# Building the S5 tables beside the first feed-forward block: T1 transposed by its filled half, its zeros written to memory once, and the table work paced anew

## The chip, the cores and the metric

The kernel runs on one core of one Trainium2 chip. The metric is device time in microseconds (us) of one execution. A core has TensorE (PE, matrix products; PEld is its weight load), VectorE (DVE), ScalarE (ACT), GpSimd (POOL) and SyncE (SP); each takes its instructions strictly in the order in which they were written for it. Transfers between memory and the core are issued on the queues of SP, ACT and POOL and share 16 DMA engines.

## The reference

A decoder trunk of two layers on 256 tokens of width 1024. Each layer is half a SwiGLU feed-forward block, a token mixer, and another half feed-forward block, all with residuals; the mixer of layer 0 is an S5 state-space layer, that of layer 1 is block-sparse attention.

```python
h = h + 0.5 * swiglu(rms_norm(h, ffn_norm[l, 0]), w_gate[l, 0], w_up[l, 0], w_down[l, 0])
h = h + mixer_l(rms_norm(h, mix_norm[l]))       # l = 0: s5_mixer, l = 1: moba_mixer
h = h + 0.5 * swiglu(rms_norm(h, ffn_norm[l, 1]), w_gate[l, 1], w_up[l, 1], w_down[l, 1])

def swiglu(h, w_gate, w_up, w_down):            # 1024 -> 2816 -> 1024
    return (silu(h @ w_gate) * (h @ w_up)) @ w_down

def s5_mixer(h, ...):                           # 64 groups of 16 channels, 64 complex states a group
    u = h @ w_in
    lam = exp((a_re + i a_im) * dt)
    bb = ((lam - 1) / (a_re + i a_im)) * (b_re + i b_im)
    st[t] = lam * st[t - 1] + bb @ u[t]         # per group, over the tokens
    y = real(c @ st) + d_skip * u
    g = gelu(y); g = g * sigmoid(g @ w_glu)
    return g @ w_out
```

Everything is float32. Of `s5_mixer`, what depends on the weights alone (powers of `lam`, their products with `b` and with `c`) is a set of tables, and this change touches how these are built.

## The kernel before

**The stages.** The phases run in the order f00 (the first feed-forward block), s5, f01, f10, moba, f11. A float32 product is done as three products of a reduced type: each weight `w` is split into `whi` (a rounded copy, by ACT, L86) and `wlo = w - whi` (by DVE, L87), activations likewise, and `mm3` (L398 to L401) adds up the three. In f00 a large matmul streams 512 columns.

**The weight stream.** `Stream` (L37 to L131) holds the order of all weights in units of 1 MB. SP loads a unit into one of three `raw` buffers (L176 for gate and up weights, L182 for down weights and others); `split` cuts a unit into two halves of `whi` and `wlo`, for which there are nine buffers. A `raw` buffer is loaded again once its second half is split. In f00 the units come by columns j of 256 hidden channels: gate and up of columns 0 and 1 (two units each), then down of column j - 1 behind gate and up of column j. `pump` calls, written between the matmuls, split ahead. SP's transfers take turns on eight semaphores, so that one can't be issued before the eighth before it has landed; POOL's do the same on eight of their own.

**Tables beside f00.** `tables` (L615) is a Python generator. While f00 is being written down, `fill(dt)` (called once per 0.7 units, three large matmuls) moves a clock `slot` and lets the generator emit work. The tables are built for 8 blocks of 8 groups. Per block b:

- `muls` and `sums` (DVE) make `zc`, products of `b` and `c` with powers of `lam`, with `cb` as their input (`b_all` makes B's part, `c_tr` transposes C on PE and ACT copies it to `cb`).
- `spread` (L850) copies `zc` on ACT to `TT` and to `MPs`, where the two groups of a pair lie in separate halves of partitions and columns and the other halves are zero, and stores `TT` to memory (`dB`, L859, on POOL). `TT` has one buffer.
- `t3_tab` (L877): 16 small matmuls, copies to `kt`, four stores to `dB` (L892, POOL).
- `t1_tab` (L863), called twice: four 128x128 transposes of `MPs` on PE (L866), a copy `t1` from PSUM on ACT (L868), one store of 256 KB to `dA` (L869, POOL). Half of what is transposed and stored is zero.

The order of it is set by lists. `LOADS` has the clock values at which the loads of B (`ld_b4`, eight pieces of 64 KB in 64-byte runs, L649) and of C (`ld_c2`, four pieces of 128 KB, L654) are put on SP's queue. `work` holds DVE's pieces with costs in units; a credit grows by `DENSE` units per unit of the clock, and a piece is emitted when the credit covers it. The PE pieces of a block (`t3_tab`, `t1_tab`, `t1_tab`) follow `LAG` = 12 units after `spread`, `PACE` = 4.0 units apart (`later`).

**After the tables.** When f00 is done, the rest of the tables is emitted, and SP loads `dA`, `dE` and `dB` of three blocks into `TA`, `TE`, `TB` (L951 to L959). The first of these waits for the last eight stores of POOL's queue. `TA` is read by the matmuls of L1009 in the S5 stage.

Of the kernel before, what the change touches and what calls it, by code (L numbers as in the profile page):

```python
# [10 lines left out]
F32 = mybir.dt.float32  # L11
F32R = mybir.dt.float32r
AF = mybir.ActivationFunctionType
# [16 lines left out]
AO = (68, 68, 68, 68)  # L30
OO = 68

LOADS = (16, 16.5, 17, 17.5, 18, 18.5, 19, 19.5, 22, 24, 26, 28)
C_AT, E_AT, B_AT, DENSE, LAG, PACE, AGE = 44, 26, 36, 0.46, 12, 4.0, 8.0


class Stream:  # L37
# [83 lines left out]
def trunk_kernel(ctx: ExitStack, tc, x, ffn_norm, ffn_w_gate, ffn_w_up, ffn_w_down, mix_norm,  # L121
# [3 lines left out]
    nc = tc.nc  # L125
# [13 lines left out]
    def psR():  # L139
        return pp.tile([128, 512], F32, name="pR", tag="R", bufs=2)  # L140
# [96 lines left out]
    ident = cst[:, 0:128]  # L237
# [7 lines left out]
    h = [h2[:, t, :] for t in range(2)]  # L245
# [374 lines left out]
    def tables(tp):  # L620

        V, P = nc.vector, nc.gpsimd

        def T(name, *shape):
            return tp.tile([128] + list(shape), F32, name=name)

        def tt(o, a, b, op, eng=V):
            eng.tensor_tensor(o, a, b, op=op)
# [4 lines left out]
            else:  # L633
                eng.tensor_scalar(o, a, s1, s2, op0=op0, op1=op1)

        MPs = [T(f"mp{k}", 2, 4, 4, 2, 16) for k in range(2)]
        TT = T("tt", 2, 4, 4, 2, 16)
        kts = [T(f"kt{k}", 7, 2, 16) for k in range(2)]
        cf7 = T("cf7", 7, 2)
        for k, n in enumerate(range(15, 1, -2)):  # L640
            for i in range(2):
                P.memset(cf7[:, k, i:i + 1], (-1.0) ** ((n - i) // 2) / math.factorial(n - i))
        for m in MPs + [TT] + kts:
            P.memset(m, 0.0)
        bn = [tp.tile([128, 32, 16], F32, name="bn", tag="n0", bufs=2) for i in range(2)]
        cn = tp.tile([128, 1280], F32, name="cn", tag="n1", bufs=2)[:, 0:1024].rearrange("p (i a c) -> p i a c", i=2, c=64)
        def ld_b4(i, c):
            b = (s5_b_re, s5_b_im)[i]
            nc.sync.dma_start(bn[i][:, 8 * c:8 * c + 8], bass.AP(tensor=b.tensor, offset=b.offset + 16384 * c,  # L649
                                                                 ap=[[16, 128], [2048, 8], [1, 16]]))  # L650

        def ld_c2(i, a):
            c = (s5_c_re, s5_c_im)[i]
            nc.sync.dma_start(cn[:, i, 4 * a:4 * a + 4], bass.AP(tensor=c.tensor, offset=c.offset + 32768 * a,  # L654
                                                                 ap=[[64, 128], [8192, 4], [1, 64]]))

        loads = [lambda i=i, c=c: ld_b4(i, c) for c in range(4) for i in range(2)]
        loads += [lambda i=i, a=a: ld_c2(i, a) for a in range(2) for i in range(2)]
        yield
        dtb = tp.tile([32, 2, 64], F32, name="dtb")  # L660
        nc.scalar.activation(dtb, ldt[:, :, None].to_broadcast([32, 2, 64]), AF.Exp)
# [1 line left out]
        ps = psR()  # L663
# [26 lines left out]
        q, y, y2, e0, e1, den = (T(n, 32) for n in ("q", "y", "y2", "e0", "e1", "den"))  # L690
# [20 lines left out]
        ps = psR()  # L711
# [118 lines left out]

        HALF = [slice(0, 64), slice(64, 128)]

        ZC = {}

        def muls(b, k):
            tt((z0, z1)[k].rearrange("p (x s n) -> p x s n", s=4, n=16),
# [3 lines left out]
        def sums(b, i):  # L840

            if i == 0:
                ZC[b] = tp.tile([128, 2, 2, 4, 80], F32, name="zc", tag="n1", bufs=2)
                P.tensor_copy(ZC[b][:, 0, :, :, 0:16].rearrange("p i q n -> p (i q) n"),
                              cb[:, b, 0].rearrange("p i q n -> p (i q) n"))
            u, v = (z.rearrange("p (m i q x) -> p m i q x", m=2, i=2, q=4) for z in (z0, z1))
            x, y = ((u[:, :, 0], v[:, :, 1]), (u[:, :, 1], v[:, :, 0]))[i]
            tt(ZC[b][:, :, i, :, 16:80], x, y, (OP.subtract, OP.add)[i])

        def spread(b):  # L850

            d_diag(b)
            tv, mv = (o.rearrange("p i q s g n -> p (i q) s g n") for o in (TT, MPs[b % 2]))
            zv = ZC[b].rearrange("p m i q (s n) -> p m (i q) s n", n=16)
            for g, r in enumerate(HALF):
                nc.scalar.activation(tv[r, :, :, g, :], zv[r, 0, :, 1:5], AF.Copy)
                nc.scalar.activation(mv[r, :, :, g, :], zv[r, 1, :, 1:5], AF.Copy)
            for i in range(2):
                nc.gpsimd.dma_start(dB[b][:, 512 * i:512 * i + 512].rearrange("p (q x) -> p q x", q=4),  # L859
                                    TT[:, i].rearrange("p q t g n -> p q (t g n)"))  # L860

        def t1_tab(b, i):
            t1 = tp.tile([128, 4, 128], F32, name="t1", tag="n0", bufs=2)  # L863
            ps = psR()
            for q4 in range(4):
                nc.tensor.transpose(ps[:, q4 * 128:(q4 + 1) * 128],  # L866
                                    MPs[b % 2][:, i, q4].rearrange("p s g n -> p (s g n)"), ident)
            nc.scalar.activation(t1.rearrange("p q c -> p (q c)"), ps, AF.Copy)  # L868
            nc.gpsimd.dma_start(dA[b][:, i * 512:(i + 1) * 512], t1.rearrange("p q c -> p (q c)"))  # L869

        DG = {}

        def d_diag(b):
            DG[b] = tp.tile([128, 2, 16], F32, name="dg", bufs=2)
            P.tensor_scalar(DG[b], i32, dT[:, b:b + 1], None, op0=OP.mult)

        def t3_tab(b):  # L877

            kt = kts[b % 2]
            ps = psR()  # L880
            zc = ZC.pop(b)
            for i in range(2):
                for qq in range(4):
                    mm(ps[32 * qq:32 * qq + 32, 0:64], MPs[b % 2][:, i, qq, 3].rearrange("p g n -> p (g n)"),
                       zc[:, 0, i, qq, 0:64], start=i == 0, stop=i == 1)
            pk = ps[:, 0:64].rearrange("p (t c) -> p t c", c=16)
            for g in range(2):
                nc.scalar.activation(kt[:, 3:7, g, :], pk, AF.Identity, scale=gm[:, g:g + 1])
            P.tensor_tensor(kt[:, 3], kt[:, 3], DG.pop(b), op=OP.add)
            for s in range(4):  # L890
                o = dB[b][32 * s:32 * s + 32, 1024:1536].rearrange("r (q x) -> q r x", q=4)
                nc.gpsimd.dma_start(o, kt[:, 3 - s:7 - s].rearrange("p t g n -> p (t g n)"))  # L892
# [12 lines left out]

        def add_spread(b):
            work.append((0.0, B_AT, (spread, b), [(t3_tab, b), (t1_tab, b, 0), (t1_tab, b, 1)], 3 * (b - 1)))

        add_e(0)
        for k, w in enumerate((1.2, 1.2, 1.4)):  # L910
# [1 line left out]
        for b in range(NB):  # L912
            for w, f in ((1.2, (muls, b, 0)), (None, b - 1), (1.2, (muls, b, 1)), (0.7, (sums, b, 0)), (0.7, (sums, b, 1))):
                if w is not None:
                    work.append((w, B_AT, f, (), 0))
                elif b:
                    add_spread(b - 1)
        add_e(1, NB - 1)
        later = [(C_AT + 1.4 * k, c_tr) + divmod(k, 2) for k in range(4)]
        done = [-4]  # L920
        dma = list(zip(LOADS, loads))
        credit, then = 0.0, slot[0]
        while work or later or dma:
# [401 lines left out]


    tab = tables(tabp) if "s5" in phases else iter(())
    next(tab, None)
    slot = [0]
# [72 lines left out]
    ps = psR()  # L1402
# [72 lines left out]
```

## Time and profile before

The time is 982.51 us (median of 3 runs, 982.28 to 982.75). The profiled execution took 982.36 us; its span, from the first to the last instruction, is 980.4 us.

| | before |
|---|---|
| profiled execution, us | 982.36 |
| span, us | 980.4 |
| PE busy, us (share) | 972.2 (99%) |
| DVE / ACT / POOL busy | 70% / 57% / 19% |
| granted TensorE clock | 0.999 |
| moved by DMA | 198.74 MB, 203 GB/s over the span |
| PE busy in 0 to 20, 20 to 40, 40 to 60 us | 19.00, 19.97, 19.11 |
| PE busy in each 20 us from 60 to 200 us | 20.00 |

The f00 stage fills about the first 220 us of the span. In the quoted rows a group reads: line, engine, operation, what it writes and reads, shape, count, busy time and mean length of one in ns, then the idle time of the engine just before, with what ended it. Matmuls overlap at their ends, so the length of one is more than the step from one to the next. The chain of work that ended last is followed back from the end; a row of it gives start, duration and instruction. Waits read: who waited for whom, microseconds in total, how often, the longest. Queue rows give packets, MB and the time of the packets as a share of 16 engines over the stretch asked for.

### The profile page before, as it was taken

Reading aid. Unit: us, or ns where it says so; the run is one execution under the profiler, and the core shown is the slowest. Engines: PE = TensorE matmul, PEld = TensorE weight load, DVE = VectorE, ACT = ScalarE, POOL = GpSimd, SP = SyncE. Lnnn points to the kernel's source line nnn. Section 1 sums busy time; section 2 is a strip of 40 time slices with the busy share of each in tenths; the row PEclk is TensorE's granted clock in tenths of the full one; section 3 lists DMA queues with packets and bytes.
Section 4 is the critical chain, followed back from the end, with each engine's and each line's share of the span. In section 5 each row is a group of like instructions: output and inputs, shape, how many; then the busy total and the mean of one; then the engine's idle time right before and its main releaser. Section 6 shows DMA issues by size and latency. Waiting matters only on the chain.

```text
span 980.4 us, 17231 instructions
## 1 busy us (share of the span) xinstructions
PE 972.2 (99%) x6727; PEld 867.5 (88%) x6727; DVE 688.8 (70%) x1118; ACT 560.4 (57%) x1008; POOL 186.5 (19%) x364
## 2 busy tenths in 40 slices
PE   9999999999999999999999999999999999999998
PEld 7878888788888999999999999998788899999997
DVE  5799767768768676666667766665789667766662
ACT  7565766553267555555456655544897556655540
POOL 6963544416511000000010000000441010000000
PEclk9999999999999999999999999999999999999999
DMA  8988877887645666565536656562544546656531
GB/s 284 249 269 279 275 261 242 298 324 245 252 173 182 213 208 215 172 212 175 172 125 214 221 173 214 173 215 92 172 145 157 186 143 214 231 174 213 172 130 44
DMA packets 140002, 198.74 MB, mean 203 GB/s; under 512 B 18232, under 2 KB 111504, under 8 KB 139664
## 3 DMA queue, kind: packets, MB, share of 16 engines
q1 hardware_dynamic: 133808, 184.32, 57.5%
q0 software_dynamic: 5536, 12.71, 3.6%
q8 instruction: 53, 0.87, 0.4%
q10 hardware_dynamic: 576, 0.61, 0.3%
q14 instruction: 29, 0.24, 0.1%
HBM read 183.89 MB, written 13.66 MB: 202 GB/s over the span
## 4 chain that ended last, share of the span: by engine, by line
PE 94%; DVE 2%; ACT 2%; issue 1%; POOL 1%; DMA 1%; SPq 0%; POOLq 0%; DVEq 0%; ACTq 0%
PE pM L554 13%; PE pM L553 13%; PE pM L555 13%; PE pA L399 9%; PE pA L401 9%; PE pA L400 9%; PE pM L399 6%; PE pM L400 6%; PE pM L401 6%; PE pA L473 1%; PE pR L1052 1%; PE pR L333 1%; DVE wlo L87 1%; PE pA L1090 1%; PE pR L866 1%
## 5 line engine op out<-in xcount | busy, mean ns | idle before, releaser
L553 PE MATMUL pM<-xa,whi 128*128 128x256 f32 x1056 | 295.7, 280 | 0.0
L554 PE MATMUL pM<-xa,whi 128*128 128x256 f32 x1056 | 294.9, 279 | 0.0
L555 PE MATMUL pM<-xa,wlo 128*128 128x256 f32 x1056 | 294.7, 279 | 0.0
L93 DVE SCALAR_TENSOR_TENSOR wlo<-raw,gT,whi 128x512 fp32r<-128x512 f32 x328 | 228.1, 748 | 71.2 <-ACT whi L92 71.0
L87 DVE TENSOR_TENSOR wlo<-raw,whi 128x1024 fp32r<-128x1024 f32 (+1 forms) x155 | 187.5, 1225 | 56.0 <-ACT whi L86 54.8
L92 ACT ACTIVATE whi<-raw,gT 128x512 fp32r<-128x512 f32 x328 | 213.7, 711 | 16.4 <-PE pA L401 14.6
L554 PEld LDWEIGHTS pM<-xa,whi 128*128 128x128 f32 x1056 | 198.5, 188 | 2.6
L553 PEld LDWEIGHTS pM<-xa,whi 128*128 128x128 f32 x1056 | 198.5, 188 | 2.3
L555 PEld LDWEIGHTS pM<-xa,wlo 128*128 128x128 f32 x1056 | 198.5, 188 | 0.0
L86 ACT ACTIVATE whi<-raw 128x1024 fp32r<-128x1024 f32 (+1 forms) x155 | 158.7, 1049 | 26.1 <-DMA raw<-in_ffn_w_up_dram 9.8
L399 PE MATMUL pA<-whi,ah 128*128 128x512 f32 x352 | 138.8, 394 | 0.0
L400 PE MATMUL pA<-wlo,ah 128*128 128x512 f32 x352 | 137.6, 391 | 0.0
L401 PE MATMUL pA<-whi,al 128*128 128x512 f32 x352 | 137.6, 391 | 0.0
L568 ACT ACTIVATE sg<-gr 128x256 f32<-128x256 f32 x66 | 27.6, 418 | 165.7 <-DVE gr L565 165.7
L399 PE MATMUL pM<-whi,xa 128*128 128x512 f32 (+1 forms) x304 | 122.2, 402 | 0.0
L400 PE MATMUL pM<-wlo,xa 128*128 128x512 f32 (+1 forms) x304 | 115.8, 381 | 0.1
L401 PE MATMUL pM<-whi,xa 128*128 128x512 f32 (+1 forms) x304 | 115.5, 380 | 0.0
L348 POOL TENSOR_TENSOR ms<-ss 128x1 f32<-128x1 f32 x10 | 1.9, 193 | 470.3 <-ACT sq L345 470.3
L401 PEld LDWEIGHTS pA<-whi,al 128*128 128x128 f32 x352 | 66.1, 188 | 14.3
L399 PEld LDWEIGHTS pA<-whi,ah 128*128 128x128 f32 x352 | 66.1, 188 | 11.6
L400 PEld LDWEIGHTS pA<-wlo,ah 128*128 128x128 f32 x352 | 66.2, 188 | 11.3
L565 DVE TENSOR_TENSOR gr<-pM,rrow 128x512 f32<-128x512 f32 x66 | 45.5, 689 | 40.9 <-PE pM L555 40.8
(269 smaller groups left out, 1214.5 us busy)
## 6 DMA issues: line engine op xcount, KB each, us to landing
raw<-in_ffn_w_down_dram SPq DMA_DIRECT2D x44, 1024.0 KB, 5.4
raw<-in_ffn_w_gate_dram SPq DMA_DIRECT2D x80, 512.0 KB, 4.0
raw<-in_ffn_w_up_dram SPq DMA_DIRECT2D x80, 512.0 KB, 5.1
raw<-in_moba_w_qkv_dram SPq DMA_DIRECT2D x12, 1024.0 KB, 5.1
TB<-dB SPq DMA_DIRECT2D x8, 768.0 KB, 6.6
raw<-in_ffn_w_gate_dram SPq DMA_DIRECT2D x16, 256.0 KB, 4.4
raw<-in_ffn_w_up_dram SPq DMA_DIRECT2D x16, 256.0 KB, 4.7
dB<-tt POOLq DMA_DIRECT2D x16, 256.0 KB, 5.1
```

What stands on the lines that cost most here:

```text
L86: nc.scalar.activation(hi[:, c], r[:, c], AF.Copy)
L87: nc.vector.tensor_tensor(lo[:, c], r[:, c], hi[:, c].bitcast(F32), op=OP.subtract)
L92: nc.scalar.activation(hi[:, c], r[:, c], AF.Identity, scale=g)
L93: nc.vector.scalar_tensor_tensor(lo[:, c], r[:, c], g, hi[:, c].bitcast(F32), op0=OP.mult, op1=OP.subtract)
L399: mm(o, xh, wh, start=start, stop=False)
L400: mm(o, xh, wl, start=False, stop=False)
L401: mm(o, xl, wh, start=False, stop=stop)
L553: mm(o, a, xh, start=k == 0 and i == 0, stop=False, skip_group_check=True)
L554: mm(o, a, xl, start=False, stop=False, skip_group_check=True)
L555: mm(o, b, xh, start=False, stop=k == 7, skip_group_check=True)
L565: V.tensor_tensor(gr, ps.rearrange("p (i c) -> p i c", i=2), Rr["row"][:, None, :].to_broadcast([128, 2, 256]), op=OP.mult)
L568: nc.scalar.activation(sg, gr[:, 0, :], AF.Silu)
```

## The change

- `MPs` (all four shifts s, zeros between) gives way to `MFs`, which holds only the last shift, for `t3_tab`. `spread` copies the block's `zc` once, dense, into `zm` (128x512).
- `t1_tab` is called once a block: four transposes of `zm` instead of eight of `MPs`, one copy `t1`. A new piece, `t1_store`, writes the result to the filled parts of `dA` in four stores of 64 KB with 256-byte runs, on POOL, instead of two of 256 KB.
- The zeros of `dA` are written by eight new transfers of 512 KB on SP's queue from a zeroed tile `blank`, at clock values 44 to 112.
- C's four pieces are loaded first, at 20 to 23; B's eight at 24 to 38. Before, B came first, at 16 to 19.5, then C at 22 to 28.
- The credit grows by 0.39 per unit up to clock 64 and by 0.46 after it (0.46 throughout before). `PACE` is 3.5 for 4.0; a block still has three later pieces.

```diff
-LOADS = (16, 16.5, 17, 17.5, 18, 18.5, 19, 19.5, 22, 24, 26, 28)
-C_AT, E_AT, B_AT, DENSE, LAG, PACE, AGE = 44, 26, 36, 0.46, 12, 4.0, 8.0
+LOADS = (20, 21, 22, 23, 24, 26, 28, 30, 32, 34, 36, 38) + (44, 50, 56, 66, 76, 88, 100, 112)
+C_AT, E_AT, B_AT, DENSE, LAG, PACE, AGE = 44, 26, 36, (64, 0.39, 0.46), 12, 3.5, 8.0
...
-        MPs = [T(f"mp{k}", 2, 4, 4, 2, 16) for k in range(2)]
+        MFs = [T(f"mf{k}", 2, 4, 2, 16) for k in range(2)]
...
-        loads = [lambda i=i, c=c: ld_b4(i, c) for c in range(4) for i in range(2)]
-        loads += [lambda i=i, a=a: ld_c2(i, a) for a in range(2) for i in range(2)]
+        loads = [lambda i=i, a=a: ld_c2(i, a) for a in range(2) for i in range(2)]
+        loads += [lambda i=i, c=c: ld_b4(i, c) for c in range(4) for i in range(2)]
+        blank = tp.tile([128, 256], F32, name="blank", bufs=1)
+        P.memset(blank, 0.0)
+        loads += [lambda b=b: nc.sync.dma_start(dA[b].rearrange("p (a c) -> p a c", a=4),
+                                              blank[:, None, :].to_broadcast([128, 4, 256])) for b in range(NB)]
...
+            ZM[b] = tp.tile([128, 8, 64], F32, name="zm", bufs=2)
+            nc.scalar.activation(ZM[b], ZC[b][:, 1, :, :, 16:80].rearrange("p i q x -> p (i q) x"), AF.Copy)
             for g, r in enumerate(HALF):
                 nc.scalar.activation(tv[r, :, :, g, :], zv[r, 0, :, 1:5], AF.Copy)
-                nc.scalar.activation(mv[r, :, :, g, :], zv[r, 1, :, 1:5], AF.Copy)
+                nc.scalar.activation(mv[r, :, g, :], zv[r, 1, :, 4], AF.Copy)
...
-        def t1_tab(b, i):
-            t1 = tp.tile([128, 4, 128], F32, name="t1", tag="n0", bufs=2)
+        def t1_tab(b):
+
+            t1 = T1[b] = tp.tile([128, 4, 128], F32, name="t1", tag="n0", bufs=2)
             ps = psR()
-            for q4 in range(4):
-                nc.tensor.transpose(ps[:, q4 * 128:(q4 + 1) * 128],
-                                    MPs[b % 2][:, i, q4].rearrange("p s g n -> p (s g n)"), ident)
-            nc.scalar.activation(t1.rearrange("p q c -> p (q c)"), ps, AF.Copy)
-            nc.gpsimd.dma_start(dA[b][:, i * 512:(i + 1) * 512], t1.rearrange("p q c -> p (q c)"))
+            zm = ZM.pop(b).rearrange("p k x -> p (k x)")
+            for k in range(4):
+                nc.tensor.transpose(ps[:, k * 128:(k + 1) * 128], zm[:, k * 128:(k + 1) * 128], ident)
+            nc.scalar.activation(t1.rearrange("p k c -> p (k c)"), ps, AF.Copy)
+
+        def t1_store(b):
+            t1 = T1.pop(b)
+            o = dA[b].rearrange("(s g n) (k q h p) -> s g n k q h p", s=4, g=2, k=4, q=2, h=2)
+            for q in range(2):
+                for g in range(2):
+                    nc.gpsimd.dma_start(o[:, g, :, :, q, g, :], t1[64 * q:64 * q + 64, :, 64 * g:64 * g + 64])
...
-                    mm(ps[32 * qq:32 * qq + 32, 0:64], MPs[b % 2][:, i, qq, 3].rearrange("p g n -> p (g n)"),
+                    mm(ps[32 * qq:32 * qq + 32, 0:64], MFs[b % 2][:, i, qq].rearrange("p g n -> p (g n)"),
...
-            work.append((0.0, B_AT, (spread, b), [(t3_tab, b), (t1_tab, b, 0), (t1_tab, b, 1)], 3 * (b - 1)))
+            work.append((0.0, B_AT, (spread, b), [(t3_tab, b), (t1_tab, b), (t1_store, b)], 3 * (b - 1)))
...
-            credit, then = min(credit + DENSE * (now - then), 1.5), now
+            credit, then = min(credit + DENSE[1 + (now > DENSE[0])] * (now - then), 1.5), now
```

More of the change, by code (lines that the diff above doesn't have):

```diff
@@ L642, in tables @@
                 P.memset(cf7[:, k, i:i + 1], (-1.0) ** ((n - i) // 2) / math.factorial(n - i))
-        for m in MPs + [TT] + kts:
+        for m in MFs + [TT] + kts:
             P.memset(m, 0.0)
@@ L831, in tables @@
         HALF = [slice(0, 64), slice(64, 128)]
-        ZC = {}
+        ZC, ZM = {}, {}
         def muls(b, k):
@@ L852, in spread @@
             d_diag(b)
-            tv, mv = (o.rearrange("p i q s g n -> p (i q) s g n") for o in (TT, MPs[b % 2]))
+            tv = TT.rearrange("p i q s g n -> p (i q) s g n")
+            mv = MFs[b % 2].rearrange("p i q g n -> p (i q) g n")
             zv = ZC[b].rearrange("p m i q (s n) -> p m (i q) s n", n=16)
+            ZM[b] = tp.tile([128, 8, 64], F32, name="zm", bufs=2)
+            nc.scalar.activation(ZM[b], ZC[b][:, 1, :, :, 16:80].rearrange("p i q x -> p (i q) x"), AF.Copy)
             for g, r in enumerate(HALF):
                 nc.scalar.activation(tv[r, :, :, g, :], zv[r, 0, :, 1:5], AF.Copy)
-                nc.scalar.activation(mv[r, :, :, g, :], zv[r, 1, :, 1:5], AF.Copy)
+                nc.scalar.activation(mv[r, :, g, :], zv[r, 1, :, 4], AF.Copy)
             for i in range(2):
@@ L860, in spread @@
                                     TT[:, i].rearrange("p q t g n -> p q (t g n)"))
-        def t1_tab(b, i):
-            t1 = tp.tile([128, 4, 128], F32, name="t1", tag="n0", bufs=2)
+        T1 = {}
+        def t1_tab(b):
+            t1 = T1[b] = tp.tile([128, 4, 128], F32, name="t1", tag="n0", bufs=2)
             ps = psR()
-            for q4 in range(4):
-                nc.tensor.transpose(ps[:, q4 * 128:(q4 + 1) * 128],
-                                    MPs[b % 2][:, i, q4].rearrange("p s g n -> p (s g n)"), ident)
-            nc.scalar.activation(t1.rearrange("p q c -> p (q c)"), ps, AF.Copy)
-            nc.gpsimd.dma_start(dA[b][:, i * 512:(i + 1) * 512], t1.rearrange("p q c -> p (q c)"))
+            zm = ZM.pop(b).rearrange("p k x -> p (k x)")
[8 more added lines that the diff above has]
+                    nc.gpsimd.dma_start(o[:, g, :, :, q, g, :], t1[64 * q:64 * q + 64, :, 64 * g:64 * g + 64])
         DG = {}
```

## The prediction

> **What bounds the kernel now.** I read the page's engine totals and its chain that ended last first: they say which engine the end waits for.
>
> ```profile
> span 980.4 us, 17231 instructions
> PE 972.2 (99%) x6727; PEld 867.5 (88%) x6727; DVE 688.8 (70%) x1118; ACT 560.4 (57%) x1008; POOL 186.5 (19%) x364
> ...
> PE 94%; DVE 2%; ACT 2%; issue 1%; POOL 1%; DMA 1%; SPq 0%; POOLq 0%; DVEq 0%; ACTq 0%
> ```
>
> PE carries 94% of the chain. An edit pays only where it takes PE work away or fills one of the few places where PE waits. The change lies in the first feed-forward block (0 to about 220 us), so the second view is the table of busy time by stretch there; columns are the stretch, its length, then busy time and instructions of PE, PEld, DVE, ACT and POOL, the granted clock, the DMA share and GB/s.
>
> ```profile
> 48.00:62.00 14.00, 13.11 (x66) 10.38 (x65) 13.96 (x23) 9.49 (x16) 13.84 (x26) 1.00 0.91 293
> 62.00:90.00 28.00, 28.00 (x129) 22.72 (x128) 26.26 (x36) 16.60 (x25) 7.24 (x9) 1.00 0.77 246
> 90.00:190.00 100.00, 100.00 (x588) 80.32 (x586) 76.99 (x110) 66.09 (x109) 47.68 (x76) 1.00 0.83 273
> ```
>
> From 62 to 190 us PE is never idle: whatever stands in PE's order there is paid for in full. Between 48 and 62 us it loses 0.89 us, with DVE and POOL full and DMA at 0.91. The third view, the chain in order of time, says why (start, duration, what).
>
> ```profile
> 36.94 1.14 DVE wlo L87
> 38.07 0.78 SPq L176
> ...
> 38.90 5.21 DMA raw<-in_ffn_w_up_dram
> ...
> 44.20 1.07 ACT whi L86
> ...
> 48.91 0.34 DVE al L500
> 49.25 0.39 DVE act L484
> ...
> 59.23 0.38 ACT cb L829
> ...
> 59.66 0.63 PE pR L826 x4
> ```
>
> and the timeline at the stall:
>
> ```profile
> 48.61 0.39 PE L401 MATMUL pM<-whi,xa 128*128 128x512 f32 x1
> ...
> 49.70 0.44 PE L497 MATMUL pR<-cst,act 128*128 128x128 f32 x2 [0.70 <-DVE act L484]
> ```
>
> A weight transfer issued at 38.90 lands 5.21 us later; ACT and DVE, which take their work in order, wait for it, then DVE is late with `act`, and PE starts its transposes at 49.70, 1.09 us after the matmul before. A usual step is 0.23, so 0.86 us are lost. A smaller loss follows at 59.66, behind the `cb` copies of the C transposes.
>
> **The change part by part.** *T1 transposes.* Eight blocks each had two calls of four transposes (64 in all); each now has one call of four (32). What four cost, in the chain:
>
> ```profile
> 97.30 0.23 PE pA L401
> 97.53 0.44 PE pR L866 x4
> 97.97 0.23 PE pA L399
> ...
> 192.24 0.44 PE pR L866 x4
> ```
>
> and by the group:
>
> ```profile
> L866 PE MATMUL pR<-cst,mp 128*128 128x128 f32 x64 | 9.6, 272 | 0.0
> ```
>
> A group of four pushes the next matmul back by 0.44 us, and the 16 groups all lie in the stretch without idle PE. Eight go: 8 x 0.44 = **-3.5 us**. The 272 ns of the group row is one transpose's own length, ends overlapping; 32 x 272 ns would be -8.7. The Trainium skill, "TensorE: Matmul & The Clock Gate", Part 4: PE-mode transpose, tells of about 275 ns for a transpose within a kernel; the trace's 272 agrees, but by that price per transpose the time would be 5.2 us lower than mine. I take the chain's step, since it is what the next matmul waits for.
>
> *Copies on ACT.* Per block ACT had two `tt` and two `mp` copies and two `t1` copies; it now has one `zm` copy (128x512), two `tt`, two quarter-size `mf` copies, one `t1`.
>
> ```profile
> L856 ACT ACTIVATE tt<-zc 64x512 f32<-64x512 f32 x16 | 10.0, 625 | 0.8 <-DVE zc L628 0.6
> L857 ACT ACTIVATE mp<-zc 64x512 f32<-64x512 f32 x16 | 9.8, 615 | 0.0
> L868 ACT ACTIVATE t<-pR 128x512 f32<-128x512 f32 x16 | 9.6, 598 | 14.4 <-PE pR L866 11.5 <-issue 1.7 <-ACT whi L92 0.5
> L888 ACT ACTIVATE kt<-pR,gm 128x64 f32<-128x64 f32 x16 | 4.1, 308 | 3.2 <-issue 1.7 <-PE pR L884 1.3
> ```
>
> Out: 2 x 615 + 598 = 1.83 us. In: about 600 for `zm` (as wide as the `t1` copy) and two of 308 to 615; nearest is the 64-wide `kt` row, 308. Net about -0.6 us a block, between -0.6 and 0. ACT is idle a third of 90 to 190 us and PE waits for it nowhere there: 0 on the path.
>
> *Stores of T1 on POOL.* Two dA stores a block become four of 64 KB in 256-byte runs. No row shows such a store; POOL's rows in 90 to 190 us and the span of single ones:
>
> ```profile
> L892 POOL DMA_DIRECT2D dB<-kt x28 | 19.7, 709 | 2.4 <-POOL kt L889 2.1 <-issue 0.3
> L859 POOL DMA_DIRECT2D dB<-tt x14 | 8.1, 578 | 8.2 <-ACT tt L856 8.2
> L869 POOL DMA_DIRECT2D dA<-t x14 | 8.0, 575 | 29.2 <-ACT t L868 29.2
> L889 POOL TENSOR_TENSOR kt<-kt,dg 128x32 f32<-128x32 f32 x8 | 6.6, 830 | 11.2 <-ACT kt L888 11.2
> L875 POOL TENSOR_SCALAR dg<-i,dT 128x32 f32<-128x32 f32 x6 | 3.6, 594 | 0.2
> L844 POOL COPY zc<-cb 128x128 f32<-128x128 f32 x6 | 1.8, 294 | 4.3 <-PE pR L884 4.3
> ...
> L892 POOL DMA_DIRECT2D dB<-kt x32: 687/704/757, 96.8 to 192.1; - x32
> ```
>
> Bounds 0.57 to 0.76 us; nearest is `dB<-kt`, also 64 KB and also scattered: 0.71. A block's other POOL work is 4 x 0.71 + 2 x 0.58 + 0.83 + 0.59 + 0.29 = 5.7 us. As built, the blocks' T3 matmuls stand 45 large matmuls apart (51 before): 45 x 0.23 = 10.4 us, and about 1 us of transposes and T3: 11.4 us. POOL needs 5.7 + 2.8 = 8.5: hidden. Behind the stores in POOL's order stand the `dB<-tt` stores, which free `tt` for the next block's ACT copies.
>
> The Trainium skill, "SBUF — State Buffer", warns in its "DVE blocks DMA" trap that a POOL-issued DMA can be held up while DVE copies, 620 ns becoming about 3100. The trace disagrees: beside a DVE 77% busy no `dB<-kt` issue took over 757 ns. By the page's 3.1 us four stores would need 12.4 us a block, 6.7 more than there is room for, and the third rival below would come about, past 1000 us.
>
> *Zero fills.* Eight writes of 512 KB each, new on SP's queue, each ahead of weight loads. As built they stand 219 to 496 large matmuls into PE's order, which is 65 to 135 us.
>
> ```profile
> q1 hardware_dynamic: 133808, 184.32, 57.5%
> ...
> ACT whi L86 <- PE pA L401: 4.6, 5, 2.2
> ACT whi L86 <- PE pM L401: 1.9, 5, 0.7
> ```
>
> The first row is the queue over the whole run: 0.575 x 980.4 / 184.32 = 3.06 us of all 16 engines per MB, so 1.6 us a fill, 12.8 in all, less half of dA's 4.2 MB later on. The idle DMA time of 65 to 135 us is 0.23 x 25 + 0.17 x 45 = 13.4 us: they fit, just. The other two rows are ACT's waits before weight splits from 66 to 200 us: only for PE, never for a transfer, so weights land before they are wanted. Cost between 0 and 12.8; I take 0, since the cover (weights landed ahead, split ahead into nine buffers) is there in the whole stretch. If the cover goes, ACT's split is late first, then PE.
>
> *C before B, spread.* As built, six of the eight B loads stood between the down weights of column 1 and the gate weights of column 3, the transfer of the 38.90 row. Now none does; C follows it, B comes one or two at a time among the next weights.
>
> ```profile
> L649 SPq DMA_DIRECT2D bn<-in_s_b_re_dram x4: 472/629/3362, 26.5 to 36.3; - x4
> L176 SPq DMA_DIRECT2D raw<-in_ffn_w_gate_dram x4: 368/412/1105, 37.8 to 54.8; - x4
> ...
> q1 hardware_dynamic: 9288, 2.27, 93.7%
> ```
>
> One B issue held SP 3.4 us, and no gate weights were issued between 30 and 37.8 us. The last row is 29 to 41 us: 9288 packets carry only 2.27 MB in 93.7% of 12 us, 11.2 us where 3.06 us per MB gives 6.9. B's 64-byte pieces thus cost 4.3 us of DMA in front of the weights. Without them that transfer can start when its buffer is free, near 34 us, and land near 39; ACT and DVE get about 5 us back before 48.6. DVE is also dealt thinner (0.39 for 0.46). The 0.86 should go whole, and half of the 0.2 at 59.66: **-0.95 us**. The 4.3 us come back at 43 to 57 us in pieces of half a microsecond, on weights by then 3 to 4 us earlier. Between nothing and 1.1; I take 0.95, and +0.1 for some new short wait.
>
> *Pace.* T1 and its store follow 3.5 units apart for 4.0: the last T1 call stands 39 large matmuls earlier, the last store 16. After the tables the loads of TA wait for POOL's last stores.
>
> ```profile
> L951 SPq DMA_DIRECT2D TA<-dA x8: 320/344/600, 200.2 to 248.8; - x8
> L1009 PE MATMUL pA<-U,TA x128: 222/222/269, 222.5 to 232.9; 128*64 128x63 f32 x128
> ```
>
> TA goes out at 200.2 and is first used at 222.5: 22 us of room: 0. SBUF and everything after the tables is as it was, 0.
>
> **The sum.** The profiled execution took 982.36 us (0.15 under the median of 982.51). 982.36 - 3.5 - 0.95 + 0.1 = **978.0 us**.
>
> **Rivals.** *First: the early stall moves, not goes.* B's pieces now meet the C transposes at 55 to 60 us; for it: ACT's `cb` copies already end last at 59.23. Against: the last C load stands 40 large matmuls, 9 us, earlier than it did. Only the transposes pay: 978.9.
>
> *Second: the fills hold the weights up.* For it: 12.8 us into 13.4 idle, DVE 94% busy at 62 to 90. Against: no wait for weights there. If the first two fills, which stand together ahead of one gate load, come through in full: +3.2, 981.2.
>
> *Third, the slower side: POOL becomes the bound of the tables.* If a T1 store costs over (11.4 - 5.7) / 4 = 1.4 us, POOL falls behind in every block, `dB<-tt` lands late, ACT stands at the next `tt` copy, and the splits and gates behind it feed PE late. At 1.57 us the loss, 0.56 a block, eats the whole gain of 4.5; at 1.8 it is 1.5 a block, 12 over eight: 990. For it: the store is the finest and the most scattered on that queue. Against: no POOL issue of 64 KB took over 0.76.
>
> *Fourth: a transpose counts in full*, 272 ns: 972.8. Against: the chain's 0.44 for four.
>
> **How the numbers follow.** Forecast 0.71, its own range 977.2 to 978.8 (a few tenths on each early wait). First 0.12, second 0.07, third 0.06, fourth 0.02, unnamed 0.02. The range of 8 in 10 goes from 977.0 to 981.3, over forecast, first and second. No change that can be told is within 0.2%, 2.0 us: faster under 980.5 (0.71 + 0.12 + 0.02 = 0.85), same 0.08, slower 0.07.
>
> **What would show it.** The profile after should have 32 T1 transposes, 8 groups of 0.44 in the chain; no PE wait at `act` near 48 us; a gate load issued near 34; no ACT wait on weights from 66 on; T1 stores near 0.7 us on POOL; TA out before 200. The prediction is wrong if ACT's waits on weights after 62 us exceed a microsecond, if PE waits at `zm` or T3, or if POOL's stores exceed 1.4 us.

## The result and the profile after

The changed kernel takes **980.92 us** (median of 22 runs, 979.27 to 983.89); before, measured beside it, 982.77 us (22 runs, 982.23 to 984.41). The ratio is 0.9983, 95% interval 0.9977 to 0.9989: 1.85 us faster, inside the predicted range, but 2.9 us above the forecast of 978.0, so less than half of the forecast gain. A time under 980.5 had been given a chance of 0.85. The profiled execution took 980.45 us, 1.91 under the one before. (In the listing above, `tables` begins at L620 and `t1_tab` at L862; the text ahead of it says L615 and L863. And f00 ends near 209 us: the 220 us given there take in the first products of S5, with `w_in`.)

The page of the changed kernel, span and engine totals:

```profile
span 978.6 us, 17165 instructions
...
PE 968.7 (99%) x6695; PEld 864.0 (88%) x6695; DVE 690.0 (71%) x1118; ACT 556.1 (57%) x1008; POOL 211.8 (22%) x381
```

PE is busy 3.5 us less and has 32 instructions fewer: the removed transposes. The span falls by only 1.8. So the work went away as planned and half of it came back as waiting. The table by stretch (same columns as in the prediction):

```profile
48.00:62.00 14.00, 13.08 (x67) 10.47 (x66) 13.97 (x21) 7.67 (x14) 13.69 (x26) 1.00 1.10 270
62.00:90.00 28.00, 28.00 (x128) 22.83 (x129) 23.57 (x32) 15.88 (x24) 6.27 (x14) 1.00 0.98 328
90.00:190.00 100.00, 100.00 (x575) 80.00 (x574) 80.80 (x115) 64.00 (x113) 77.56 (x98) 1.00 0.97 282
```

From 62 to 190 us PE is still never idle. DMA's share went from 0.77 and 0.83 to 0.98 and 0.97, and POOL's busy time from 47.68 to 77.56 us. What PE waits for between 30 and 245 us (total, times, longest), before:

```profile
PE pR L497 <- DVE act L484: 0.7, 1, 0.7
PE pR L826 <- ACT cb L829: 0.2, 1, 0.2
```

and after:

```profile
PE pM L399 <- ACT us L1015: 1.3, 1, 1.3
PE pR L830 <- DVE al L500: 0.9, 1, 0.9
```

The two early waits of before are gone. A new one of 0.9 us stands ahead of C's transposes, and one of 1.3 us stands in S5, at about 218 us, where before there was none.

**Where the 1.3 us come from.** ScalarE's timeline at the start of S5 tells it (start, duration, instruction, idle time before it and its releaser). The first `xa` follows the last work of f00; `us` empties a PSUM buffer that PE needs for its next product; the two splits `whi` of the last `w_in` unit stand between two `us` in ACT's order. Before:

```profile
208.75 0.60 ACT L335 ACTIVATE xa<-pR 128x512 fp32r<-128x512 f32 x1 [3.12 <-PE pR L333]
...
218.42 0.45 ACT L999 ACTIVATE us<-pM,rr 128x256 f32<-128x256 f32 x1
219.84 1.34 ACT L92 ACTIVATE whi<-raw,gT 128x512 fp32r<-128x512 f32 x2 [0.97 <-DMA raw<-in_s_w_in_dram]
221.09 0.46 ACT L999 ACTIVATE us<-pM,rr 128x256 f32<-128x256 f32 x1
```

After:

```profile
204.99 0.60 ACT L335 ACTIVATE xa<-pR 128x512 fp32r<-128x512 f32 x1 [3.12 <-PE pR L333]
...
214.66 0.46 ACT L1015 ACTIVATE us<-pM,rr 128x256 f32<-128x256 f32 x1
217.35 1.33 ACT L92 ACTIVATE whi<-raw,gT 128x512 fp32r<-128x512 f32 x2 [2.23 <-DMA raw<-in_s_w_in_dram]
218.59 0.45 ACT L1015 ACTIVATE us<-pM,rr 128x256 f32<-128x256 f32 x1
```

f00 ends 3.76 us earlier (208.75 to 204.99): nearly all of the forecast 4.35 had been gained there. (This end moves from one execution to the next: 208.75 and 209.49 in two profiles with the f00 of before, 204.69 to 205.51 in four with the f00 of after. A single difference of this kind is good to some 0.8 us.) But ACT was already waiting 0.97 us for that `w_in` unit **before** the change. The second `us` of before ends at 221.55, and PE's next product starts at 221.60, in PE's own timeline of before:

```profile
221.60 0.39 PE L399 MATMUL pM<-whi,xa 128*128 128x256 f32 x1
```

Not a wait on PE's account, but no slack either. After, the unit is split 2.49 us earlier (219.84 to 217.35), and S5's matmul starts 2.51 us earlier, at 219.09. The gain that passed is that of the transfer, not that of PE. The chain of waits of the changed kernel runs over it:

```profile
204.44 12.88 DMA raw<-in_s_w_in_dram
...
218.68 0.37 ACT us L1015
...
219.09 0.38 PE pM L399
```

And SP's queue says why the transfer came no sooner. Before:

```profile
200.18 0.35 SPq L951 DMA_DIRECT2D TA<-dA  x1
...
203.82 1.87 SPq L959 DMA_DIRECT2D TB<-dB  x3
205.80 0.38 SPq L188 DMA_DIRECT2D raw<-in_s_w_in_dram  x1
```

After:

```profile
198.76 0.35 SPq L967 DMA_DIRECT2D TA<-dA  x1
...
202.24 2.09 SPq L975 DMA_DIRECT2D TB<-dB  x3
204.44 0.64 SPq L188 DMA_DIRECT2D raw<-in_s_w_in_dram  x1
```

The unit stands on SP behind three TA, three TE and three TB loads, 4.6 MB, and the first TA waits for POOL's last stores. Those stores let TA out only 1.42 us earlier, though PE was 3.76 earlier. The rows of the T1 store, over the whole run and, for the four issued from 184 to 199 us, with the median time from issue to landing:

```profile
L885 POOL DMA_DIRECT2D dA<-t x32: 987/1250/1671, 104.6 to 190.7; - x32
...
dA<-t POOLq DMA_DIRECT2D x4, 64.0 KB, 8.8
```

One issue takes 1.25 us at the median and up to 1.67. The last four land 8.8 us after their issue; the three dA stores of before in that stretch took 2.5 to 5.7 us. So the last store went out 6.8 us earlier than before (190.68 for 197.50), but most of that was lost in the landing. Right ahead of these stores on POOL's queue stands the last store of `dE`, 1040 KB, issued at 186.81 and landed 8.2 us later; in the kernel before it landed in 5.9 us, the T1 store right behind it in 5.7, and the last one, 4.7 us behind it, in 2.5. Whether `dE` holds the T1 stores up, or the traffic holds up both, no run separates, since none moves `dE`.

### The profile page after: what moved, and what is told of

Its sections match the earlier page's. It is cut to its first block, busy times and chain, and to the rows that moved or that the text cites. A ratio compares the mean times of both kernels' runs of the same rounds, so it can differ in the third digit from the quotient of the medians.

```text
span 978.6 us, 17165 instructions
## 1 busy us (share of the span) xinstructions
PE 968.7 (99%) x6695; PEld 864.0 (88%) x6695; DVE 690.0 (71%) x1118; ACT 556.1 (57%) x1008; POOL 211.8 (22%) x381
## 4 chain that ended last, share of the span: by engine, by line
PE 88%; DVE 4%; POOL 2%; DMA 2%; ACT 2%; issue 1%; SPq 0%; ACTq 0%; POOLq 0%
PE pM L554 13%; PE pM L553 13%; PE pM L555 13%; PE pA L399 9%; PE pA L401 9%; PE pA L400 9%; PE pM L399 6%; PE pM L400 5%; PE pM L401 5%; DVE wlo L87 2%; DMA raw<-in_s_w_in_dram 1%; PE pR L1068 1%; POOL sc L686 1%; PE pA L1106 1%; PE pR L333 1%
## 5 line engine op out<-in xcount | busy, mean ns | idle before, releaser
L553 PE MATMUL pM<-xa,whi 128*128 128x256 f32 x1056 | 295.7, 280 | 0.0
L553 PEld LDWEIGHTS pM<-xa,whi 128*128 128x128 f32 x1056 | 198.5, 188 | 2.3
```

What stands on the lines that cost most here:

```text
L553: mm(o, a, xh, start=k == 0 and i == 0, stop=False, skip_group_check=True)
```

## The experiments

The theory after the comparison, A: f00 gained what was forecast, less some tenths early on; at S5 PE is held by the `w_in` unit behind TA, TE and TB on SP's queue, so what passes is the move of POOL's last T1 stores. The rival, B: something of T1 itself (late stores, fills, the clock) costs the time, wherever the unit stands in the queue. Each ratio is against runs of the kernel before beside it, with the 95% interval.

**The changed kernel again.**

> The changed kernel once more, as the mark for the runs beside it. Both theories: about 1.8 us under the kernel before, PE waiting some 0.9 us before the C transposes near 61 us and 1.3 us at the first products of S5 near 218 us, the wait that the profile gives to ACT's split of the last w_in unit.

Measured: 980.47 us (11 runs, 979.28 to 983.30), ratio 0.9983 (0.9975 to 0.9992): the result stands. The profile this time fell on a longer execution, span 981.5 us. Its wait in S5:

```profile
PE pM L399 <- ACT us L1015: 1.8, 1, 1.8
```

and its stretch just behind the S5 wait (last three columns: granted clock, DMA share, GB/s):

```profile
222.00:232.00 10.00, 10.00 (x111) 8.93 (x109) 7.87 (x14) 4.30 (x9) 4.76 (x4) 0.83 0.73 238
```

In the first profile of the changed kernel the clock there is 1.00 and PE has 179 instructions in it, here 0.83 and 111. Taken by the microsecond it is 0.50 from 222 to 225 us and 1.00 again from 226: a mean of 0.83 over 10 us is 3.4 us at half clock. So a longer wait costs a second time. The runs on record show the same: of the 22 of the changed kernel six have a mean clock of 0.997 or 0.998 and take 982.08 to 983.89 us, and the sixteen at 0.999 or above take 979.27 to 981.67.

**TB's loads out of the way.** TB is loaded after S5's steps t0, t1 and t2, and no longer at the end of `tables`:

```diff
             ld_a(b)
             ld_e(b)
-        for b in range(3):
-            ld_b(b)
...
                 {"t": t1, "r": rot, "y": y_out, "g": g_tr}[name[0]](int(name[1]))
+                if word in ("t0", "t1", "t2"):
+                    ld_b(int(word[1]))
```

> Three TB loads (2.4 MB) leave the place on SP's queue ahead of the last w_in unit and go out behind the T1 products of S5. Theory A (PE's lead from f00 is given back because the last w_in unit stands behind 4.6 MB of table loads, which themselves wait for POOL's last stores): by 3.06 us per MB that unit lands about 7 us earlier, near 210; the wait of 1.3 us at S5's start goes, the time is 1.2 to 1.4 us under the changed kernel, about 3.1 under before. Theory B (the transfers as a whole are saturated by fills and fine stores, and whatever is moved comes late elsewhere): the wait stays or reappears at the first use of TB near 231 us, the time stays within 0.5 us of the changed kernel.

Measured: **978.66 us** (5 runs, 978.45 to 978.78), ratio 0.996 (0.9947 to 0.9973). SP's queue and PE's waits from 30 to 245 us:

```profile
198.44 0.35 SPq L964 DMA_DIRECT2D TA<-dA  x1
...
201.99 0.86 SPq L188 DMA_DIRECT2D raw<-in_s_w_in_dram  x1
```

```profile
PE pR L830 <- DVE al L500: 0.9, 1, 0.9
```

TA goes out when it did; the unit is issued 2.45 us earlier, lands in 9.0 us for 12.88, the S5 wait is gone, and so is the spread of the times; no run has a mean clock under 0.999. The time is 1.81 us below the changed kernel measured beside it (980.47), and 2.26 below the 980.92 of the first measurement: more than the 1.2 to 1.4 expected. Part of that is the clock: the eight runs at full clock of the changed kernel beside it have a median of 980.27, 1.6 us above; the rest was not followed. A is borne out: T1's stores let TA out as late as in the changed kernel, and without the queue in between they cost nothing.

**The same in the kernel before.** The same edit on the kernel before the change.

> The kernel before, with the three TB loads moved behind the T1 products of S5. It has no wait at S5's start that the move could take away. Theory A: within 0.3 us of before. Theory B: if the TB loads hold up something else there, 1 us or more faster.

Measured: 982.56 us (10 runs, 982.09 to 983.16), ratio 0.9996 (0.9987 to 1.0005). The room is worth nothing there, since PE reached the place just when the unit did. (The profile is of the longest of the ten runs, 983.16 us: a wait of 1.5 us at `act`, where the kernel before has 0.7, put the end of f00 at 209.49, ahead of anything that the edit touches.)

**T1's transposes twice.** Each call does its four transposes two times:

```diff
-            for k in range(4):
+            for k in (0, 1, 2, 3) * 2:
```

> Every T1 call does its four transposes twice, into the same place. f00 gets 8 x 0.44 = 3.5 us longer. Theory A: the last w_in unit lands when it did, so the 1.3 us wait at S5's start goes with the lead; net +2.2 us against the changed kernel, so about 0.4 over before. Theory B: the wait stays, net +3.5. If a transpose cost its full 272 ns, f00 would get 8.7 us longer.

Measured: 983.48 us (11 runs, 982.62 to 985.17), ratio 1.0012 (1.0003 to 1.0021). A group in the chain:

```profile
102.15 0.87 PE pR L877 x8
```

Eight take 0.87, four 0.44: 0.11 each, not 0.27. f00 ends at 208.60 for 204.99, 3.6 us later, which is the price of eight groups of 0.44. Against the changed kernel measured beside it (980.47) the time is 3.0 us up, between the 2.2 of theory A and the 3.5 of theory B. The S5 wait shrank only to 0.7 us: TA went out at 201.75 for 198.76, since the stores moved out with f00, and the wait is tied to them more than to PE.

**T1 stored from SP.** The four stores of a block on SP's queue instead of POOL's:

```diff
-                    nc.gpsimd.dma_start(o[:, g, :, :, q, g, :], ...)
+                    nc.sync.dma_start(o[:, g, :, :, q, g, :], ...)
```

> The four T1 stores of a block go to SP's queue. POOL loses 32 issues of 1.25 us. Theory A: the last stores land sooner, the table loads start 1 to 3 us earlier than at 198.8, and the wait at S5's start falls by as much, to 0 to 0.3; 1 us under the changed kernel. Theory B: the stores take as long on this queue, weight loads behind them start later, and the time is the same or up to 2 us longer.

Measured: 990.29 us (6 runs, 989.81 to 995.22), ratio 1.0085 (1.007 to 1.01). I had expected at most 2 us more. On SP's queue one issue takes 1.61 us at the median and up to 6.64; the last four occupy SP from 193.76 to 203.36, TA goes out at 206.25 for 198.76, and the unit behind it at 212.00. PE's S5 wait:

```profile
PE pM L399 <- ACT us L1015: 8.7, 1, 8.7
```

It doesn't tell A from B, since it moved the unit and the stores at once. It does show the same place taking 8.7 us, and a clock of 0.50 from 221.3 to 231.5 us, which is 4.1 us past the end of the wait at 227.4.

**One coarse store.** T1 goes to memory as one store of 256 KB in 2 KB runs. Its elements then stand in wrong places of `dA`; the amount stored and the program after it stay the same.

```diff
-            for q in range(2):
-                for g in range(2):
-                    nc.gpsimd.dma_start(o[:, g, :, :, q, g, :], t1[64 * q:64 * q + 64, :, 64 * g:64 * g + 64])
+            nc.gpsimd.dma_start(dA[b][:, 0:512], t1.rearrange("p k c -> p (k c)"))
```

> The changed kernel with one T1 store a block of 256 KB in 2 KB runs in place of four scattered ones of 64 KB; T1 then stands in the wrong places, so the output is not the reference's. Theory A, sharpened (the last scattered stores take 8 to 9 us to land, and the table loads with the last w_in unit behind them start on that landing): the issue costs POOL about 0.57, the last store lands 3 to 4 us sooner, TA goes out at about 195, the wait at S5's start goes, 1.3 us under the changed kernel. If only the order behind the table loads matters and the stores do not: the wait stays at 1.3 us.

Measured: 978.54 us (5 runs, 978.22 to 979.58), ratio 0.9957 (0.9943 to 0.9971). The store's group on POOL from 90 to 190 us, and SP's queue:

```profile
L882 POOL DMA_DIRECT2D dA<-t x8 | 4.7, 589 | 2.5 <-ACT t L878 2.3 <-issue 0.2
```

```profile
196.68 0.35 SPq L964 DMA_DIRECT2D TA<-dA  x1
...
202.53 0.48 SPq L188 DMA_DIRECT2D raw<-in_s_w_in_dram  x1
```

One issue of 0.59 us takes the place of four of 1.25, TA goes out 2.08 us earlier and the unit 1.91 earlier, and the S5 wait is gone with TB where it was. So the wait has two handles: what stands between TA and the unit (TB), and how early POOL is done with T1. The landing itself hardly changed: the last store, issued at 187.46, needed 9.0 us. It is the issue time that the fine runs cost; the landing is slow at 188 to 198 us for either form, and for a 256 KB store of the kernel before, in the run that follows, too (9.1 to 9.9 us). In both these runs, too, the T1 stores stand right behind `dE`, which took 9.0 and 9.8 us to land.

**New loads, spread and pace alone**, on the kernel before, with T1 as it was.

```diff
-LOADS = (16, 16.5, 17, 17.5, 18, 18.5, 19, 19.5, 22, 24, 26, 28)
-C_AT, E_AT, B_AT, DENSE, LAG, PACE, AGE = 44, 26, 36, 0.46, 12, 4.0, 8.0
+LOADS = (20, 21, 22, 23, 24, 26, 28, 30, 32, 34, 36, 38)
+C_AT, E_AT, B_AT, DENSE, LAG, PACE, AGE = 44, 26, 36, (64, 0.39, 0.46), 12, 3.5, 8.0
```

(C's loads first, and the credit line as in the change.)

> Loads in the new order and at the new clock values, the two densities and 3.5, with T1 as before (eight transposes, two coarse stores, no fills). The early wait moves (0.9 at 48.6 goes, about 1.0 comes before the C transposes at 61): f00 -0.2. Theory A: coarse stores land within 6 us and earlier than before, no wait at S5's start: 982.2 to 982.6, within 0.3 us of before. Theory B: the wait at S5's start is here too, 1 us or more slower than before.

Measured: 982.77 us (11 runs, 982.33 to 983.66), ratio 0.9998 (0.9989 to 1.0007). PE's waits:

```profile
PE pR L826 <- DVE al L500: 1.0, 1, 1.0
PE pM L399 <- ACT us L999: 0.9, 1, 0.9
```

The time is as theory A has it, within 0.3 us of before, but A's reason is out: there is a wait at S5's start. The wait at `act` goes and one of 1.0 us at C's transposes comes, as in the changed kernel. f00 ends only 0.33 us earlier (first `xa` at 208.42 for 208.75), where 0.95 less 0.1 was forecast; 0.33 lies within what this end moves between executions, so that no gain there is shown. The `w_in` split starts at 220.44, 0.60 later than before, and with it S5. Although the last T1 store was issued at 191.69 instead of 197.50, TA went out at 200.99, after the 200.18 of before: it landed 9 us later, where that of before took 2.5.

**T1 alone**: the T1 part and the fills, with `LOADS`, 0.46 and `PACE` 4.0 of before.

> The T1 part alone (four transposes, fine stores, zero fills) with B first, the old clock values of the loads, 0.46 throughout and pieces 4.0 apart. Theory A: f00 is 3.5 us shorter, with the two early waits of the kernel before (0.9 at 48.6, 0.2 at 59); the last T1 store stands later by about 16 large matmuls (3.7 us) than in the changed kernel, so the last w_in unit lands later and the wait at S5's start grows to 3 us or more, past which the clock falls to half for some 3.4 us; 982 to 985, no better than before. Theory B (what was lost, was lost to the new loads and pace): no wait at S5's start, 979 to 980.

Measured: 985.70 us (11 runs, 982.82 to 987.05), ratio 1.0024 (1.0014 to 1.0033): with 32 transposes fewer it is slower than before, by a little more than theory A allowed, and theory B is out. f00 ends at 204.97, as early as in the changed kernel. Then PE's waits, the chain, and the stretch behind:

```profile
PE pM L399 <- ACT us L1015: 5.0, 1, 5.0
```

```profile
207.15 13.91 DMA raw<-in_s_w_in_dram
```

```profile
222.00:232.00 10.00, 9.17 (x103) 8.46 (x103) 8.10 (x13) 4.20 (x9) 1.69 (x2) 0.83 0.63 226
```

At `PACE` 4.0 the last T1 stores are issued at 190.4 to 194.4 instead of 187.4 to 190.7; TA goes out at 201.43, the unit at 207.15, and PE, 3.78 us early, waits 5.0 us and then has a clock of 0.83 (0.50 from 222.8 to 226.2 us). So the new pace, costed at nothing, or what came with it, is what makes the T1 part worth anything as long as TB stands in front of the unit. The run puts back the order of the loads and the spread as well; that it is the pace is argued from the issue times, since no run changed `PACE` alone.

**T1 alone, with TB out of the way**; beside it the changed kernel with TB late once more, as the mark.

> T1's 32 transposes for 64, its fills and its finer stores, with the loads, the spread and the pace of before, and the TB loads moved out of the table stage. Theory A: the wait at the start of S5, 5.0 us in the profile of the T1 part alone, goes, and the 3.8 us that its table stage had gained by then stay: before less 3.6 to 3.8, about 979.0 us (range 978.4 to 979.6). Then the new order, spread and pace are worth about 0.3 us together once TB is out of the way. Theory B (T1's late stores, and not the queue order, make the wait): TA is what S5 waits for, the wait stays over 1 us and the time over 981.

> The changed kernel with the TB loads moved out of the table stage, a second time, as the mark for the other two kernels run beside it. Theory A (the changed kernel's loss is the w_in unit standing behind TA, TE and TB on SP's queue) expects the first measurement back: 978.66 us within 0.3, TensorE without a wait between 190 and 230 us.

Measured: T1 alone with TB late 979.47 us (8 runs, 979.05 to 980.29), ratio 0.9969 (0.9958 to 0.9979); the mark 978.93 us (5 runs, 978.38 to 979.14), ratio 0.9963 (0.9951 to 0.9976). The same edit that gave the kernel before nothing takes 6.2 us from T1 alone (985.70 to 979.47, from two sets of runs in which the kernel before differs by 0.4). Theory B, a wait of over 1 us at S5 and a time over 981, is out: PE's waits of T1 alone with TB late are all early,

```profile
PE pR L497 <- DVE act L484: 1.0, 2, 0.8
PE pR L877 <- ACT kt L904: 0.6, 1, 0.6
```

and sum to 1.6 us, where the mark has 0.9. The new order, spread and pace are worth about 0.5 us (979.47 less 978.93) once nothing hides them; the two intervals overlap, so the 0.5 is not sure.

**Spread thinner**: TB late, and 0.33 for 0.39.

```diff
-C_AT, E_AT, B_AT, DENSE, LAG, PACE, AGE = 44, 26, 36, (64, 0.39, 0.46), 12, 3.5, 8.0
+C_AT, E_AT, B_AT, DENSE, LAG, PACE, AGE = 44, 26, 36, (64, 0.33, 0.46), 12, 3.5, 8.0
```

> The changed kernel with the TB loads moved, and the spread set to 0.33 instead of 0.39, so that fewer pieces are dealt before the early stages end. If the wait of 0.92 us ahead of C's transposes near 61 us is made by the pieces that fill VectorE's queue there, it shrinks or goes: 977.7 to 978.2 us. Rival (the first of the prediction, once more): the work put off comes back as another wait in the table stage, and the time is 978.6 or above.

Measured: 980.98 us (11 runs, 979.76 to 982.02), ratio 0.9983 (0.9974 to 0.9991), 2.05 us worse than the mark. PE's waits:

```profile
PE pR L497 <- DVE act L484: 0.5, 1, 0.5
PE pR L497 <- ACT kt L904: 0.4, 1, 0.4
PE pR L877 <- DVE al L500: 0.3, 1, 0.3
PE pR L877 <- ACT kt L904: 0.2, 1, 0.2
```

The wait ahead of C's transposes is gone, so the pieces in DVE's queue did make it. But the work put off comes back as four waits later in the stage, 1.4 us, and f00 ends at 206.69 for 204.69 in the first profile with TB late. (The listed waits account for 0.5 of these 2.0 us; the rest was not traced.) ACT's list names what backs up: from 62 to 200 us `tt` waits 15.2 us for the stores `dB<-tt` that free its buffer, where TB late alone has 3.3. That is the path that the prediction's third rival named. The value of 0.39 is the better one. Leaving the fills out was not tried, since `dA` would then be read unwritten.

What the profiles say of one place, beside the medians (first `xa`: end of f00; split: ACT's start on the last `w_in` unit):

| kernel | first `xa`, us | TA issued | split | PE waits in S5 | median, us |
|---|---|---|---|---|---|
| before | 208.75 | 200.18 | 219.84 | 0 | 982.77 |
| loads and pace alone | 208.42 | 201.0 | 220.44 | 0.9 | 982.77 |
| T1 alone | 204.97 | 201.43 | 221.09 | 5.0 | 985.70 |
| changed | 204.99 | 198.76 | 217.35 | 1.3 | 980.92 |
| coarse store | 205.05 | 196.68 | (not late) | 0 | 978.54 |
| changed, TB late | 204.69 | 198.44 | (not late) | 0 | 978.66 |

Each row but the last column is one profiled execution. Where PE waits at S5, its matmul starts 1.74 or 1.75 us after the split does, whatever f00 gained. (T1 alone: 222.83 against 221.09; changed: 219.09 against 217.35.)

## Why the prediction was right and where it failed

*T1 transposes, -3.5.* Right. The chain has eight groups of four, of 0.44 us:

```profile
102.03 0.44 PE pR L877 x4
...
183.22 0.44 PE pR L877 x4
```

and doubling them cost 3.6 us in f00. The fourth rival, 272 ns for each transpose, is out: the group row's length is no step.

*Copies on ACT, 0.* Right: ACT's busy time from 90 to 190 us went from 66.09 to 64.00 us, and PE waits nowhere there.

*Stores of T1, 0.71 within 0.57 to 0.76.* Wrong: 0.99 to 1.67, median 1.25. The nearest row was chosen by its KB (`dB<-kt`, 64 KB). Yet one store of 256 KB in 2 KB runs costs 0.59; what fits is the number of runs (64 KB in 256-byte runs are 256, 256 KB in 2 KB runs are 128), which I did not vary by itself. Of the 29.9 us by which POOL's busy time from 90 to 190 us rose, the T1 stores are 23.7 (31.7 for 8.0). Other POOL work got longer too, for a reason that no run isolates: `dB<-tt` from 578 to 847 ns each, `dg` from 594 to 1672, the `zc` copies from 294 to 929; with the coarse store they take 589, 936 and 616. The third rival's limit of 1.4 us was not crossed on the mean (1.30 in the group from 90 to 190 us), POOL had 22 us of 100 left, and no block fell behind in a way that PE felt: the sign set at 1.4 us was passed by single stores only, and it is not what cost the time. What the price did was to delay the last block's stores.

*Zero fills, 0.* Right for PE: no wait from 62 to 190 us. Wrong in its reason. ACT does wait for weights now, with DMA at 0.97 to 0.98:

```profile
ACT whi L86 <- DMA raw<-in_ffn_w_up_dram: 4.5, 3, 3.3
```

The sign of being wrong that was set on these waits, one microsecond, is passed, and yet PE doesn't wait there: the splits run far enough ahead of it. So the first half of the second rival came about, its price not. The fills alone don't make these waits: of the ten profiles with fills six show them for f00's weights (up to 9.3 us in all, from 62 to 200 us), four, T1 twice, T1 alone and the coarse store among them, show none, and of the three without fills none does. How much of the slack is left was not measured.

*C before B and the spread, -0.95 + 0.1.* Half right. The gate load went out at 33.68 (34 was predicted) and the wait at `act` is gone. In its place stands the first rival's wait, with another engine than named: not ACT's `cb` copies but DVE, busy 10.39 of the 12 us from 36 to 48 and 13.97 of the 14 from 48 to 62, which comes late with `al`, and C's transposes stand behind that in PE's order.

```profile
58.24 1.29 DVE z L628 x2
59.54 1.18 DVE wlo L87
60.72 0.81 DVE e L628 x2
61.52 0.34 DVE al L500
...
61.91 0.63 PE pR L830 x4
```

Table products (`z`, `e`) and weight splits lie just before `al`; with the spread at 0.33 this wait goes. From 48 to 62 us PE is busy 13.08 us, before 13.11: the early stall moved and did not shrink. The term of 0.85 was mis-sized: 0.33 us in f00, within the movement between executions.

*Pace, "22 us of room: 0".* This is the step that failed. With it fails the line "everything after the tables is as it was, 0", which passes all of f00's gain on to the end. The room was measured to TA's own first use, and there it is true (TA first used at 220.0 in the changed kernel, issued at 198.76). The queue behind it was left out: on SP the last `w_in` unit stands behind TA, TE and TB, and that unit had no room at all, since ACT was waiting 0.97 us for it already and PE started within 0.05 us of what it released. In its place the runs show that the unit's split moved by only 2.49 us where f00 moved by 3.76, and that PE waits 1.28 us, about the difference. The sign "TA out before 200" came true and was the wrong thing to look for.

Put together: f00 gains 3.76 (forecast 4.35). At S5 2.51 of it pass, close to the 2.49 that the unit's split moved by, and the profiled execution ends 1.91 us earlier; the last 0.6 go in small pieces: the first and the last of the feed-forward matmuls behind S5 (L553, at 308.6 and 965.2 us) both come 2.2 us earlier than before, so 0.3 are lost between S5's start and there, and the rest behind the last of them. Of the missing 2.45 us between forecast and profile, 0.6 are the early stages, 1.25 the S5 wait, and 0.6 those pieces; only the S5 wait is larger than what f00 moves between executions. The runs show the S5 part in two ways: 1.8 us come back when TB is moved (980.47 to 978.66), and 2.4 against the first measurement when the stores are coarse (980.92 to 978.54). That 980.92 lies in the range at all is luck: the upper end, 981.3, was set for early stalls and fills that hold up the weights, not for this wait.

The version to keep is the changed kernel with TB's loads behind t0 to t2: 978.66 and 978.93 us in two sets of runs, 3.5 to 3.8 us under the kernel before measured beside it. That this comes near 978.0 does not bear the forecast out, which was made for another kernel.

## What to carry over

When a stage is shortened, look at the first transfer that the *next* stage waits for, and at every issue ahead of it on its queue: a wait that lies on ACT alone, with PE starting right behind it, is a bound with no slack, though PE's list of waits is empty. A room has to be measured for everything that stands behind the moved thing on its queue, not for the thing itself. The price of a store on POOL did not follow its KB here; its number of runs fits better.

## What the runs showed of the hardware

- A store of 64 KB in 256-byte runs took POOL 0.99 to 1.67 us to issue, one of 256 KB in 2 KB runs 0.59, `dB<-kt` of 64 KB 0.71.
- T1 stores issued on POOL from 187.4 to 194.4 us, behind the 1040 KB store of `dE` (7.3 to 9.8 us to land), took 6.8 to 9.9 us to land, fine or coarse. In the kernel before, where `dE` landed in 5.9, the two behind it took 5.7 and 2.5.
- The granted clock fell to 0.50 for 3.4 us after a PE wait of 1.8 us (from 221.9 us on) and after one of 5.0 (from 222.8 on), and for 10.2 us around one of 8.7 (from 221.3 on, 2.6 us into the wait). It stayed at 1.00 after waits of 0.7, 0.9 and 1.3 us. The Trainium skill, "TensorE: Matmul & The Clock Gate", Part 1, puts the limit at idle gaps of more than about 3.4 us; the wait of 1.8 us lies below that. Whether the thin work just around the wait counts as idle too, no run here shows.
